# Sine products of the rotation and norm weights of queries and keys on VectorE instead of GpSimd

## The chip, the cores and the metric

The kernel runs on one core of a Trainium2 chip. The metric is the device time of one execution in microseconds, the median of several runs. The engines are TensorE (PE, matmuls; PEld is its weight load), VectorE (DVE), ScalarE (ACT), GpSimd (POOL) and SyncE (SP), which issues the transfers.

## What is computed

Two layers of a hybrid block over 1024 latent tokens and 256 context tokens, width 1024, float32. Each layer norms and modulates its input and projects it with one wide matrix; three mixers work on the result and a second matrix adds their output to the residual. The mixers are differential attention (four heads, two maps of 64 dimensions each, values of 128), a state space scan (16 heads) and a retention scan (4 heads). The two steps that the change touches, cut from the reference:

```
def rms_norm(x, gain):                       # per head and map, over 64 dimensions
    return x * rsqrt(mean(x * x) + EPS) * gain

def apply_rope(x, cos, sin):                 # x1, x2: halves of the last axis
    return concatenate([x1 * cos - x2 * sin, x1 * sin + x2 * cos])

q_l = apply_rope(rms_norm(aq, attn_q_norm), cos, sin)      # attention, per head
k_l = apply_rope(rms_norm(ak, attn_k_norm), cos, sin)
k_c = rms_norm(ak_c, attn_k_norm)                          # context: no rotation
q, k = apply_rope(rq, cos, sin), apply_rope(rk, cos, sin)  # retention: no norm
```

## The kernel before

Tokens lie on partitions in ten tiles of 128 (eight latent, two context). Every dense product is computed in three matmuls: weights and activations are split in a high part (`wh`, `ah`, rounded on ScalarE) and a rest (`wl` on GpSimd, `al` on VectorE or GpSimd; `split`, L280 to 284), and `mm3` (L301 to 312) sums high by high, high by rest and rest by high in one PSUM buffer. There are two such buffers (`ps_mm`), so a third dense tile waits until the first has been copied out. The projection is a generator (`dense_all`, L1332) that yields after each PSUM tile. The mixers are generators too, and `phase` (L392) draws dense tiles between a mixer's steps by a budget per phase, so that TensorE has dense matmuls between the short ones of a mixer. This sets only the order in which instructions are written; a scheduler then reorders them per engine by its own estimate of when each is ready, and each engine runs its list in order.

`two_units` (L342) makes 128 columns each of two units (such as q0 and q1): tile by tile, ScalarE copies the first unit out of PSUM, VectorE the second (`copy`, L118). `head_prep` (L945) takes one head's k and q: `qk_norm` (L931) sums the squares, forms the inverse root on VectorE, multiplies by it (L942) and then by the gain (L943); `rope` (L916) works in two pieces of four tiles: a sine product into `rm` (L924), a cosine product in place (L925), and a difference and a sum of half width (L928, L929). Context tokens are normed but not rotated. Then k is split again (`khl`, L958) and transposed. The first head is prepared in a phase of its own, the next three inside the loop of the head before.

`head_loop` (L1045) runs over blocks of 128 queries. For each of two maps, `head_b` makes the scores (L986), their maxima on VectorE (`mx`, L988), the negated maximum of all (`nb`, L993) and the exponentials on ScalarE (L998); `head_c1` subtracts the second map from the first on VectorE (`rho`, L1013, one element per partition, and the update of `e`, L1016, up to 1280 columns); then follow transposes (L149) and the product with the values (L1037). `ret_mix` (L1108) calls `rope` for rk and rq of two retention heads, four times in all.

GpSimd also makes the rests of the weights (L284), products of the scan (L766, L895, L901) and of retention (L1141, L1167).

Of the kernel before, what the change touches and what calls it, by code (L numbers as in the profile page):

```python
# [13 lines left out]
ALU = mybir.AluOpType  # L14
# [4 lines left out]
P = 128  # L19
# [33 lines left out]
class Net:  # L53
# [862 lines left out]
    def rope(self, x):  # L916
        nc = self.nc
        for i in range(0, NLT, 4):
            t = slice(i, i + 4)
            m = self.work("rm", (P, 4, 4, 32))  # L920
            x4 = x[:, t, :].rearrange("p t (a e) -> p t a e", e=32)
            sb = self.sin[:, t].unsqueeze(2).to_broadcast([P, 4, 4, 32])
            cb = self.cos[:, t].unsqueeze(2).to_broadcast([P, 4, 4, 32])
            nc.gpsimd.tensor_tensor(out=m, in0=x4, in1=sb, op=ALU.mult)  # L924
            nc.vector.tensor_tensor(out=x4, in0=x4, in1=cb, op=ALU.mult)  # L925
            xh = x[:, t, :].rearrange("p t (a s e) -> p t a s e", s=2, e=32)
            mh = m.rearrange("p t (a s) e -> p t a s e", s=2)
            nc.vector.tensor_tensor(out=xh[:, :, :, 0], in0=xh[:, :, :, 0], in1=mh[:, :, :, 1], op=ALU.subtract)  # L928
            nc.vector.tensor_tensor(out=xh[:, :, :, 1], in0=xh[:, :, :, 1], in1=mh[:, :, :, 0], op=ALU.add)  # L929

    def qk_norm(self, x, gain, nt):  # L931
        nc = self.nc
        ss = self.tiny("qss", 2 * NT)
        for i in range(0, nt, 4):
            n = min(4, nt - i)
            sq = self.work("qsq", (P, n, P))
            nc.scalar.activation(out=sq, in_=x[:, i:i + n], func=AF.Square)
            nc.vector.tensor_reduce(out=ss[:, 2 * i:2 * i + 2 * n],
                                    in_=sq.rearrange("p t (m d) -> p (t m) d", m=2), axis=AX.X, op=ALU.add)
        r = self.mean_rsqrt(ss[:, 0:2 * nt], 2 * nt, 64)  # L940
        xv = x[:, 0:nt].rearrange("p t (m d) -> p (t m) d", m=2)
        nc.vector.tensor_tensor(out=xv, in0=xv, in1=r.unsqueeze(2).to_broadcast([P, 2 * nt, 64]), op=ALU.mult)  # L942
        nc.gpsimd.tensor_tensor(out=xv, in0=xv, in1=gain.unsqueeze(1).to_broadcast([P, 2 * nt, 64]), op=ALU.mult)  # L943

    def head_prep(self, h, last):  # L945
        nq = NLT if last else NT
# [619 lines left out]
```

## Time and profile before

| | |
|---|---|
| median of 3 runs | 2859.97 us (2858.49 to 2863.67) |
| profiled execution | 2862.42 us |
| its span in the profile | 2860.6 us, 45098 instructions |
| TensorE busy | 2668.0 us (93%) |
| VectorE busy | 1774.1 us (62%) |
| ScalarE busy | 1058.0 us (37%) |
| GpSimd busy | 775.3 us (27%) |
| mean granted clock of TensorE | 0.964 of full speed |

The span is that of the profiled instructions; the profiled execution took 1.8 us more in all. Times in the rows below are counted from the start of the span. A shape is partitions x elements; buffer numbers are left out of names. A bracket behind a row of a timeline holds the engine's idle time just before it and what ended that.

### The profile page before, as it was taken

The numbers are of one execution on the slowest core, as the hardware profiler recorded it, in microseconds if no ns is written. First come the engines' busy times: TensorE is split into PE (matmuls) and PEld (weight loads), VectorE is DVE, ScalarE is ACT, GpSimd is POOL, SyncE is SP. The second block draws the span as 40 slices with busy tenths as digits, with TensorE's granted clock in tenths as the row PEclk, the third lists the DMA queues.
The fourth block names the chain that finished last, engine by engine and source line by source line (L and its number), as shares of the span: only waits on it lengthen the run. The fifth ranks groups of instructions, "written<-read, shape, count | busy, mean of one in ns | idle before, by whom it ended". The sixth has DMA issues, their size and how long they took to land.

```text
span 2860.6 us, 45098 instructions
## 1 busy us (share of the span) xinstructions
PE 2668.0 (93%) x17116; PEld 2342.0 (82%) x17116; DVE 1774.1 (62%) x4213; ACT 1058.0 (37%) x2678; POOL 775.3 (27%) x688
## 2 busy tenths in 40 slices
PE   7689999999999999998999989998999999999999
PEld 4578877888888799986878777877988888889787
DVE  5567657656677775656455666667567767564651
ACT  3443323224444545332233443332244544442330
POOL 2333323232111121233231423223421221022540
PEclk8789999999999999998999999998999999999999
DMA  6012212222111111123543112112210010002461
GB/s 245 10 46 73 69 48 74 80 69 83 47 58 45 54 30 34 33 91 110 168 166 95 29 48 71 54 50 66 60 30 16 23 29 24 23 18 67 139 210 56
DMA packets 111832, 196.04 MB, mean 69 GB/s; under 512 B 13600, under 2 KB 43104, under 8 KB 111616
## 3 DMA queue, kind: packets, MB, share of 16 engines
q1 hardware_dynamic: 111616, 193.17, 21.2%
q8 instruction: 135, 2.21, 0.3%
q14 instruction: 81, 0.66, 0.1%
HBM read 155.43 MB, written 37.68 MB: 68 GB/s over the span
## 4 chain that ended last, share of the span: by engine, by line
PE 77%; DVE 12%; DMA 4%; ACT 3%; issue 2%; POOL 2%; SPq 0%; DVEq 0%; ACTq 0%; POOLq 0%
PE mm L310 34%; PE mm L312 18%; PE t L149 5%; PE o L1037 4%; PE s L986 4%; PE s L822 2%; PE s L772 2%; DVE mx L988 2%; PE o L815 1%; DMA mr<-mix 1%; PE t L793 1%; ACT e L998 1%; DVE e L1016 1%; PE mm L541 1%; DMA wa<-in_wa_dram 1%
## 5 line engine op out<-in xcount | busy, mean ns | idle before, releaser
L310 PE MATMUL mm<-ah,wh 128*128 128x512 f32 (+1 forms) x1680 | 630.4, 376 | 12.9 <-DVE xr L1234 6.0
L310 PE MATMUL mm<-al,wh 128*128 128x512 f32 (+1 forms) x1680 | 623.9, 371 | 0.9 <-DVE al L284 0.9
L310 PE MATMUL mm<-ah,wl 128*128 128x512 f32 (+1 forms) x1680 | 622.7, 371 | 0.0
L284 POOL TENSOR_TENSOR wl<-raw,wh 128x512 fp32r<-128x512 f32 x224 | 293.6, 1332 | 762.1 <-ACT wh L282 731.9
L312 PE MATMUL mm<-wh,ah 128*128 128x256 f32 x1568 | 454.4, 290 | 8.7 <-DVE q L118 7.0
L312 PE MATMUL mm<-wl,ah 128*128 128x256 f32 x1568 | 449.3, 287 | 0.5 <-POOL wl L284 0.5
L312 PE MATMUL mm<-wh,al 128*128 128x256 f32 x1568 | 448.5, 286 | 0.0
L310 PEld LDWEIGHTS mm<-ah,wh 128*128 128x128 f32 x1680 | 323.0, 192 | 68.7 <-issue 5.6
L310 PEld LDWEIGHTS mm<-ah,wl 128*128 128x128 f32 x1680 | 322.9, 192 | 50.8 <-issue 0.7
L310 PEld LDWEIGHTS mm<-al,wh 128*128 128x128 f32 x1680 | 323.6, 193 | 49.8 <-DVE al L284 1.5
L312 PEld LDWEIGHTS mm<-wh,ah 128*128 128x128 f32 x1568 | 301.7, 193 | 15.3 <-DVE q L118 7.8
L998 ACT ACTIVATE e<-s,nb 128x512 f32<-128x512 f32 (+1 forms) x384 | 232.1, 614 | 200.7 <-DVE nb L993 197.5
L312 PEld LDWEIGHTS mm<-wl,ah 128*128 128x128 f32 x1568 | 301.7, 192 | 3.5 <-POOL wl L284 0.9
L312 PEld LDWEIGHTS mm<-wh,al 128*128 128x128 f32 x1568 | 301.6, 192 | 1.9
L988 DVE TENSOR_REDUCE mx<-s 128x1 f32<-128x512 f32 (+1 forms) x400 | 225.1, 589 | 58.5 <-PE s L986 56.8
L986 PE MATMUL s<-kT,qT 128*128 128x512 f32 (+1 forms) x800 | 217.9, 379 | 16.6 <-ACT e L998 15.2
L282 ACT ACTIVATE wh<-raw 128x512 fp32r<-128x512 f32 x224 | 130.5, 627 | 214.9 <-PE mm L310 88.5
L1037 PE MATMUL o<-v,aT 128*128 128x128 f32 x1312 | 176.7, 277 | 0.4 <-DVE aT L118 0.4
L1037 PEld LDWEIGHTS o<-v,aT 128*128 128x128 f32 x1312 | 165.3, 193 | 5.2 <-DVE mx L988 0.8
L986 PEld LDWEIGHTS s<-kT,qT 128*128 128x128 f32 x800 | 136.2, 195 | 40.3 <-ACT e L998 25.0
L794 ACT ACTIVATE t<-t 128x512 f32<-128x512 f32 x144 | 82.1, 582 | 159.4 <-PE t L793 155.3
L766 POOL TENSOR_TENSOR xw<-xn,dtpk 128x512 f32<-128x512 f32 (+2 forms) x96 | 79.5, 840 | 213.2 <-PE s L772 102.1
(281 smaller groups left out, 4543.0 us busy)
## 6 DMA issues: line engine op xcount, KB each, us to landing
raw<-in_wi_dram SPq DMA_DIRECT2D x176, 256.0 KB
wa<-in_wa_dram SPq DMA_DIRECT2D x48, 512.0 KB
E<-cume SPq DMA_DIRECT2D x144, 128.0 KB
mr<-mix SPq DMA_DIRECT2D x64, 256.0 KB
raw<-in_wo_dram SPq DMA_DIRECT2D x32, 256.0 KB
x<-xr SPq DMA_DIRECT2D x26, 256.0 KB
mix<-cv SPq DMA_DIRECT2D x8, 640.0 KB
mix<-sg SPq DMA_DIRECT2D x8, 640.0 KB
```

Source lines behind the costliest of these rows:

```text
L149: self.nc.tensor.transpose(ps[:, j * P:(j + 1) * P], srcs[i + j], self.ident)
L282: nc.scalar.activation(out=hi, in_=x, func=AF.Copy)
L284: e.tensor_tensor(out=lo, in0=x, in1=hi.bitcast(F32), op=ALU.subtract)
L310: nc.tensor.matmul(ps, lhsT=w, rhs=x, start=st, stop=sp)
L312: nc.tensor.matmul(ps, lhsT=x, rhs=w, start=st, stop=sp)
L766: nc.gpsimd.tensor_tensor(out=xw, in0=xn[:, a:a + m].rearrange("p t (h e) -> p t h e", h=2), in1=self.wend[:, a:a + m, h0:h0 + 2].unsqueez ...
L772: nc.tensor.matmul(ps[:, j * P:(j + 1) * P], lhsT=bn[:, c, :], rhs=xw[:, j].rearrange("p h e -> p (h e)"), start=True, stop=True)
L794: nc.scalar.activation(out=ps, in_=ps, func=AF.Exp)
L986: nc.tensor.matmul(ps[:, 0:n], lhsT=qT[:, 2 * m + s, :], rhs=kT[m][:, t0:t0 + n], start=(s == 0), stop=(s == 1))
L988: nc.vector.tensor_reduce(out=mx[:, ci:ci + 1], in_=ps[:, 0:n], axis=AX.X, op=ALU.max, negate=len(chunks) == 1)
L998: nc.scalar.activation(out=em[:, t0:t0 + n], in_=pss[ci][:, 0:n], func=AF.Exp, bias=nb, accum_out=z[:, 3 * m + ci:3 * m + ci + 1])
L1037: nc.tensor.matmul(po[:, 0:P], lhsT=aT[j], rhs=v[:, j, :], start=(j == b0), stop=(j == NT - 1))
```

## The change

The sine product of `rope` and the gain product of `qk_norm` are issued on VectorE instead of GpSimd. They read and write the same tiles; no other line is edited.

```
             cb = self.cos[:, t].unsqueeze(2).to_broadcast([P, 4, 4, 32])
-            nc.gpsimd.tensor_tensor(out=m, in0=x4, in1=sb, op=ALU.mult)
+            nc.vector.tensor_tensor(out=m, in0=x4, in1=sb, op=ALU.mult)
             nc.vector.tensor_tensor(out=x4, in0=x4, in1=cb, op=ALU.mult)
...
         nc.vector.tensor_tensor(out=xv, in0=xv, in1=r.unsqueeze(2).to_broadcast([P, 2 * nt, 64]), op=ALU.mult)
-        nc.gpsimd.tensor_tensor(out=xv, in0=xv, in1=gain.unsqueeze(1).to_broadcast([P, 2 * nt, 64]), op=ALU.mult)
+        nc.vector.tensor_tensor(out=xv, in0=xv, in1=gain.unsqueeze(1).to_broadcast([P, 2 * nt, 64]), op=ALU.mult)
```

The scheduler writes another order for all engines from the first head on. Three places follow. The first is GpSimd's list where the first head is prepared; `k_726` is that head's k, `wl_5158` the rest of the weights of the next dense tiles, `wl_5193` that of the ones after; rows with a minus stand only before.

```order
 L766 TENSOR_TENSOR xw_4997<-xn_4296,dtpk_503 128x384
-L943 TENSOR_TENSOR k_726_4592<-k_726_4592,keep_269 128x1280
 L284 TENSOR_TENSOR wl_5158<-raw_5159,wh_5157 128x512
 L284 TENSOR_TENSOR wl_5158<-raw_5161,wh_5157 128x512
 L284 TENSOR_TENSOR wl_5158<-raw_5163,wh_5157 128x512
-L924 TENSOR_TENSOR rm_5456<-k_726_4592,sin 128x512
-L924 TENSOR_TENSOR rm_5461<-k_726_4592,sin 128x512
 L284 TENSOR_TENSOR wl_5158<-raw_5165,wh_5157 128x512
 L284 TENSOR_TENSOR wl_5193<-raw_5194,wh_5192 128x512
```

The three products are gone from the list; the fourth split of `wl_5158` follows the third directly.

The second place is VectorE's list there; `q_804` is a unit of q that is being copied out of PSUM. Before:

```order
L118 COPY adar_5176<-mm_5167 128x512
L826 SCALAR_TENSOR_TENSOR cv_3817<-cv_3817,cols_113,o_5106 128x256
L834 TENSOR_TENSOR cv_3817<-cv_3817,s_5107 128x256
L925 TENSOR_TENSOR k_726_4592<-k_726_4592,cos 128x512
L242 SCALAR_TENSOR_TENSOR ada_148<-t_5178,cols_113 128x8
L834 TENSOR_TENSOR cv_3817<-cv_3817,s_5107 128x256
L928 TENSOR_TENSOR k_726_4592<-k_726_4592,rm_5456 128x8x32
L929 TENSOR_TENSOR k_726_4592<-k_726_4592,rm_5456 128x8x32
L925 TENSOR_TENSOR k_726_4592<-k_726_4592,cos 128x512
L284 TENSOR_TENSOR khl_5556<-k_726_4592,khl_5556 128x4x64
L928 TENSOR_TENSOR k_726_4592<-k_726_4592,rm_5461 128x8x32
L929 TENSOR_TENSOR k_726_4592<-k_726_4592,rm_5461 128x8x32
```

The first copy of `q_804` is the row after these. With the change, from the same copy of `adar_5176` on:

```order
L118 COPY adar_5176<-mm_5167 128x512
L924 TENSOR_TENSOR rm_5456<-k_726_4592,sin 128x512
L924 TENSOR_TENSOR rm_5461<-k_726_4592,sin 128x512
L834 TENSOR_TENSOR cv_3817<-cv_3817,s_5093 128x256
L925 TENSOR_TENSOR k_726_4592<-k_726_4592,cos 128x512
L118 COPY q_804_5203<-mm_5204 128x128
L925 TENSOR_TENSOR k_726_4592<-k_726_4592,cos 128x512
L826 SCALAR_TENSOR_TENSOR cv_3817<-cv_3817,cols_113,o_5106 128x256
L928 TENSOR_TENSOR k_726_4592<-k_726_4592,rm_5456 128x8x32
```

Both sine products stand in front, and the first copy of `q_804` stands between the two cosine products instead of behind the rope.

The third place is VectorE's list where the q of head 1 is normed and rotated inside the loop of head 0; `mx_6925` and `nb_6938` are the maxima of one block of scores, `e_6743` the exponentials that the block before updates, `v_1107` a unit that is copied out of PSUM. Before:

```order
L942 TENSOR_TENSOR q_804_5203<-q_804_5203,ry_6713 128x1280
L988 TENSOR_REDUCE mx_6925<-s_6926 128x1
L1007 TENSOR_REDUCE zs_6944<-z_6727 128x2
L988 TENSOR_REDUCE mx_6925<-s_6930 128x1
L118 COPY v_1107_6845<-mm_6846 128x128
L1011 RECIPROCAL rz_6946<-zs_6944 128x2
L118 COPY v_1107_6845<-mm_6897 128x128
L988 TENSOR_REDUCE mx_6925<-s_6934 128x1
L1013 SCALAR_TENSOR_TENSOR rho_6948<-zs_6944,nlam_280,rz_6946 128x1
L993 TENSOR_REDUCE nb_6938<-mx_6925 128x1
L1016 SCALAR_TENSOR_TENSOR e_6743<-e_6826,rho_6948,e_6743 128x1280
L925 TENSOR_TENSOR q_804_5203<-q_804_5203,cos 128x512
```

With the change:

```order
L942 TENSOR_TENSOR q_804_5203<-q_804_5203,ry_6713 128x1280
L988 TENSOR_REDUCE mx_6925<-s_6926 128x1
L943 TENSOR_TENSOR q_804_5203<-q_804_5203,keep_269 128x1280
L1007 TENSOR_REDUCE zs_6944<-z_6727 128x2
L988 TENSOR_REDUCE mx_6925<-s_6930 128x1
L118 COPY v_1107_6845<-mm_6846 128x128
L118 COPY v_1107_6845<-mm_6897 128x128
L988 TENSOR_REDUCE mx_6925<-s_6934 128x1
L924 TENSOR_TENSOR rm_6887<-q_804_5203,sin 128x512
L924 TENSOR_TENSOR rm_6892<-q_804_5203,sin 128x512
L1011 RECIPROCAL rz_6946<-zs_6944 128x2
L993 TENSOR_REDUCE nb_6938<-mx_6925 128x1
```

The gain product stands between the maxima and ahead of both v copies, the sine products ahead of `nb_6938`; behind these rows come the rest of the rope and only then the update of `e_6743`.

## Rows read from the trace of the kernel before

**Rows 1.** The page: busy us, share of the span, instructions of each engine.

```profile
PE 2668.0 (93%) x17116; PEld 2342.0 (82%) x17116; DVE 1774.1 (62%) x4213; ACT 1058.0 (37%) x2678; POOL 775.3 (27%) x688
```

**Rows 2.** The page: the chain that ended last, shares of the span by engine.

```profile
PE 77%; DVE 12%; DMA 4%; ACT 3%; issue 2%; POOL 2%; SPq 0%; DVEq 0%; ACTq 0%; POOLq 0%
```

**Rows 3.** Busy us by stretch: PE, PEld, DVE, ACT, POOL, clock, DMA, GB/s.

```profile
550.00:650.00 100.00, 94.08 (x721) 88.02 (x720) 56.12 (x138) 27.30 (x69) 28.03 (x16) 0.97 0.25 81
650.00:1155.00 505.00, 480.57 (x3447) 432.52 (x3447) 350.91 (x835) 238.63 (x721) 90.82 (x58) 0.98 0.16 51
2100.00:2555.00 455.00, 427.39 (x3032) 393.08 (x3031) 318.00 (x758) 218.94 (x664) 81.22 (x53) 0.98 0.08 24
```

**Rows 4.** VectorE's groups by form, the norm: busy, mean ns.

```profile
L942 DVE TENSOR_TENSOR k<-k,ry 128x1280 f32<-128x1280 f32 x8 | 11.9, 1488 | 0.1
L942 DVE TENSOR_TENSOR q<-q,ry 128x1024 f32<-128x1024 f32 x4 | 4.9, 1222 | 0.1
```

**Rows 5.** The cosine product's line: ns least, median, most; first, last start.

```profile
L925 DVE TENSOR_TENSOR k<-k,cos x16: 670/684/1748, 579.9 to 2363.1; 128x512 f32<-128x512 f32 x16
```

**Rows 6.** GpSimd's groups by form, the moved products: busy, mean ns.

```profile
L943 POOL TENSOR_TENSOR k<-k,keep 128x1280 f32<-128x1280 f32 x8 | 23.6, 2946 | 157.1 <-DVE k L942 73.5 <-PE t L149 38.6 <-DVE nb L993 31.7
L924 POOL TENSOR_TENSOR rm<-q,sin 128x512 f32<-128x512 f32 x16 | 26.6, 1684 | 0.6
```

**Rows 7.** Timelines at 878 us, GpSimd and VectorE: start, us, instruction.

```profile
878.31 3.00 POOL L943 TENSOR_TENSOR q<-q,keep 128x1280 f32<-128x1280 f32 x1 [36.06 <-DVE q L942]
878.41 2.92 DVE L1013 SCALAR_TENSOR_TENSOR rho<-zs,nlam,rz 128x1 f32<-128x1 f32 x1
```

**Rows 8.** VectorE's timeline, the same two lines, GpSimd idle.

```profile
714.54 0.21 DVE L1013 SCALAR_TENSOR_TENSOR rho<-zs,nlam,rz 128x1 f32<-128x1 f32 x1
715.32 1.54 DVE L1016 SCALAR_TENSOR_TENSOR e<-e,rho,e 128x1280 f32<-128x1280 f32 x1
```

**Rows 9.** VectorE's timeline, first and last row on a moved product.

```profile
579.94 1.58 DVE L925 TENSOR_TENSOR k<-k,cos 128x512 f32<-128x512 f32 x1
2552.43 2.65 DVE L1016 SCALAR_TENSOR_TENSOR e<-e,rho,e 128x1280 f32<-128x1280 f32 x1
```

**Rows 10.** VectorE's groups by form, two products of two SBUF inputs.

```profile
L799 DVE TENSOR_TENSOR mt<-mt,t 128x512 f32<-128x512 f32 x72 | 49.2, 684 | 0.4
L284 DVE TENSOR_TENSOR al<-mr,ah 128x512 fp32r<-128x512 f32 x32 | 36.9, 1166 | 14.6 <-ACT ah L282 14.4
```

**Rows 11.** TensorE's timeline, dense tiles of q, idle time in brackets.

```profile
576.64 0.38 PE L312 MATMUL mm<-wh,ah 128*128 128x256 f32 x1 [0.22 <-DVE zu L364]
590.02 0.58 PE L312 MATMUL mm<-wh,ah 128*128 128x256 f32 x1 [5.70 <-DVE q L118]
```

**Rows 12.** VectorE's timeline there.

```profile
585.99 3.10 DVE L284 TENSOR_TENSOR khl<-k,khl 128x256 fp32r<-128x256 f32 x1
589.68 0.28 DVE L118 COPY q<-mm 128x128 f32<-128x128 f32 x1
```

**Rows 13.** GpSimd's timeline there.

```profile
578.44 2.53 POOL L924 TENSOR_TENSOR rm<-k,sin 128x512 f32<-128x512 f32 x2
580.91 4.61 POOL L284 TENSOR_TENSOR wl<-raw,wh 128x512 fp32r<-128x512 f32 x3
```

**Rows 14.** ScalarE's timeline there, the fourth split's first half.

```profile
579.26 0.63 ACT L282 ACTIVATE wh<-raw 128x512 fp32r<-128x512 f32 x1 [4.06 <-DMA raw<-in_wi_dram]
```

**Rows 15.** Busy us behind that stall, columns as in rows 3.

```profile
590.00:599.70 9.70, 9.68 (x61) 9.69 (x62) 2.65 (x9) 4.78 (x12) 5.21 (x3) 0.73 0.31 105
```

**Rows 16.** TensorE's timeline at the rope of rk.

```profile
1312.28 1.12 PE L149 MATMUL t<-ident,rk 128*128 128x128 f32 x4 [4.63 <-DVE rk L929]
```

**Rows 17.** TensorE's timeline, two waits for the e update.

```profile
884.18 0.63 PE L149 MATMUL t<-ident,e 128*128 128x128 f32 x4 [0.76 <-DVE e L1016]
965.58 1.07 PE L149 MATMUL t<-ident,e 128*128 128x128 f32 x8 [2.12 <-DVE e L1016]
```

**Rows 18.** TensorE's timeline at the q of head 1.

```profile
740.79 0.39 PE L312 MATMUL mm<-wh,ah 128*128 128x256 f32 x1 [0.74 <-DVE v L118]
```

## The prediction

> **What bounds the kernel now.** I read the busy times first, then the chain of waits, then the busy times by stretch, and last the timelines at the places where the moved products stand. TensorE is busy for 2668.0 of 2860.6 us, so that 192.6 us are all that any reordering of other engines could give; VectorE follows with 1774.1 us, GpSimd has 775.3 us in all [rows 1]. In the chain that ended last TensorE holds 77%, VectorE 12%, GpSimd 2% [rows 2]. The reader is to see two things in this: GpSimd is not what the kernel waits for, and VectorE is the engine that the change loads and the second on the chain. By stretch: where the first head is prepared (550 to 650 us) TensorE is busy for 94.1 of 100 us; in the head loops of layer 0 for 480.6 of 505 us with VectorE at 350.9, in those of layer 1 for 427.4 of 455 with VectorE at 318.0 [rows 3]. VectorE is thus at 69 to 70% where twelve of the sixteen norms run, and TensorE still idles some 5% there.
>
> **What moves, and its gross price on VectorE.** Sixteen gain products (one per norm of k or q, two layers of four heads) and 48 sine products (two per rope; eight k, eight q, four rk and four rq). The gain product has the form of the line ahead of it: a whole k or q times a broadcast operand. That line takes 1.488 us on 1280 columns and 1.222 us on 1024 [rows 4]; twelve of the first and four of the second make 17.9 + 4.9 = 22.8 us. The sine product has the form of the cosine product, 0.684 us [rows 5]: 48 x 0.684 = 32.8 us. Gross: +55.6 us on VectorE. Off GpSimd go products of 2.95 us and of about 1.3 us each (a mean of 1.68 where they waited) [rows 6]; with GpSimd at 27% this is worth nothing by itself. No DMA is issued by either line, so no queue of transfers is moved; the order that the scheduler writes changes on all engines from the first head on.
>
> **What VectorE gets back.** The profile shows the two engines in each other's way. At 878.31 us GpSimd begins a gain product of 3.00 us; VectorE's next instruction, one element per partition, lasts 2.92 us and ends with it [rows 7]. The same line takes 0.21 us, and the e update behind it 1.54 us, where GpSimd is idle [rows 8]. I went through the VectorE rows that lie on one of the 64 products: 23 of them are longer than their form alone, by 23.2 us together; the first (1.58 for 0.68 us) and the last (2.65 for 1.54 us) are shown [rows 9]. That goes. The Trainium skill, page "SBUF — State Buffer", section "Who interferes with whom", says that a VectorE instruction with two SBUF inputs contends with a GpSimd instruction that reads SBUF, and that the one that comes later waits for the whole of the other; the rows of 878 us agree. By that page the change also has a price: the 64 products have two SBUF inputs on VectorE as well, and meet the weight splits that stay on GpSimd.
> How much the 64 products are held up on VectorE I bound from rows: the sum of two masks (512 columns, two SBUF inputs) means 0.684 us over 72, no stall at all; the splits of the mix loads, made while GpSimd does the same, mean 1.166 us over 32, 0.48 more [rows 10]. So 64 products pay between 0 and 31 us. I take 0.1 us each, 6 us, nearer to the first, since in the head loops GpSimd is left with little (90.8 of 505 us now, the moved products among it [rows 3]). Net on VectorE: 55.6 + 6 - 23 = **+38 us**. If all 64 met a split, the worst that the page's rule allows here, the net were 64 us, and the time by the sum below 2860.
>
> **What of it reaches the end.** Of 38 us I count VectorE's share of the chain, 12%: **+4.6 us**. Bounds: 0, if TensorE's dense matmuls cover all of it, and 18 us, the slower rival below.
>
> **First place, the head prepared at 575 to 590 us.** Here TensorE stands still for 5.70 us until a copy of q frees its PSUM buffer [rows 11]. In the order before, GpSimd has two sine products ahead of the fourth split of the same weights: they occupy it from 578.44 to 580.91, and the split follows at once [rows 13], though its input was on its way from 579.26 [rows 14]. The order on TensorE starts the next q tile while it waits, so both tiles end together, and VectorE reaches the first q copy only behind the cosine products and a split of k that lasts 3.10 us [rows 12]. After the change nothing of the head stands ahead of that split on GpSimd, the first q tile is finished first, and its copy stands between the two cosine products. Worked out: the split's input is ready at 579.26 + 0.63 = 579.9, the split (4.61 / 3 = 1.5 us) at 581.4. A matmul takes 9.7 x 0.73 / 61 = 0.116 us at full clock [rows 15]. TensorE starts the tile at 576.64 [rows 11], has done 18 of its 24 matmuls at 578.7 and waits 2.7 us for the split. In the 13.4 us from 576.64 to 590.02 it works 13.4 - 5.7 = 7.7 us; the same work with the new wait ends at 587.0, when the first copy is long made: **-3.0 us**. Behind the stall the granted clock is 0.73 over 9.7 us [rows 15], so partly at the lower of its two levels (1.2 and 2.4 GHz), which costs 9.7 x 0.27 = 2.6 us; a wait of 2.7 us remains, so I count half: **-1.3 us**.
>
> **Second place, the rope of rk at 1307 to 1312 us.** TensorE waits 4.63 us for the last line of the rope [rows 16], while GpSimd makes sine products. In the new order the sine products stand in front on VectorE, and TensorE's next instructions are dense matmuls that wait for two residual updates instead of the rope. The bounds are 0 and -4.6. I take **-1.0 us**, near 0, because three of the four sine products (0.684 us each) stand ahead of the first of those updates.
>
> **Third place, attention.** Two waits of TensorE for the e update, 0.76 us at 884.18 and 2.12 us at 965.58 [rows 17], lie right behind such hold-ups; I count **-2.0** of their 2.9 us. On the other side the products now stand in front of the softmax. At the q of head 1 the gain product comes between the maxima, and in front of the v copies: TensorE waits there 0.74 us already [rows 18], and that grows by the 1.49 us of the product. The two sine products stand ahead of the negated maximum and the whole rope ahead of the e update, which comes later by at least 1.49 + 4 x 0.684 = 4.2 us, less the stalls that end. Two tiles of dense matmuls (2 x 24 x 0.116 = 5.6 us) stand on TensorE for that time; they start when the v copies are made. The loss is the wait for those copies, at most 1.5 us, and lies inside the 4.6 us above.
>
> **Sum.** -3.0 - 1.3 - 1.0 - 2.0 + 4.6 = -2.7 us. The profiled execution took 2862.4 us (1.8 around its span; 2.45 above the median of the runs, 2859.97): 2859.7 for one like it, and **2857** for the median. What a measurement of this kernel can tell from no change is about 0.2%, 5.7 us.
>
> **Rivals.**
> 1. The softmax pays (slower). The scheduler puts a ready product ahead of the negated maximum and the e update; while GpSimd had them, they ran in the gaps. Twelve norms lie in head loops; if each costs TensorE the 1.49 us of its gain product, that is 18 us in place of 4.6: 2857 + 13 = 2870. From 0.6 us per norm on (7.3 us) the change is slower than before, from 1.1 on by more than 0.2%. For it: the wait at 740.79, VectorE at 70%. Against it: TensorE is 94 to 95% busy in the head loops with dense matmuls to fill in [rows 3].
> 2. The stalls weighed more than I count. Both first places lose their stalls and clock falls whole (5.7 + 2.6 + 4.6), the e waits go (2.9), and VectorE's net load is covered: -16 us, 2844. For it: VectorE's stalls come in the middle of in-order chains. Against it: the new order keeps waits at both places.
> 3. TensorE hides it all, and the first place only changes its wait (weights instead of a PSUM buffer): 2859 to 2861. For it: 93% busy. Against it: 5.7 us of plain idle that the order explains.
> Beside these the order changes in places that have nothing to do with the products; that adds a few us of either sign, which is in the ranges.
>
> **How the numbers follow.** Forecast 0.50, rival 1 0.24, rival 2 0.17, rival 3 0.09. The forecast's own range is 2849 to 2863; about 0.22 of its 0.50 lie below 2854.3, the rest within 0.2%. Rival 2 is faster, rival 1 slower, rival 3 two thirds within and one third slower. Faster 0.39, same 0.34, slower 0.27. The range for 8 in 10 reaches from short of all of rival 2 with favourable reordering, 2839, to just above rival 1, 2872.
>
> **What would show it.** Right: VectorE's busy time near 1812 us, GpSimd's near 660; the one-element line near 0.21 us at all places; no wait of 5 us for a q copy near 585; the rope's wait near 1310 shorter. Wrong: waits of TensorE for v copies, e or the maxima grown by over 10 us in the head loops (rival 1), or VectorE's busy time above 1830 us, its products stalled by the splits. A time above 2866 or below 2849 refutes the sum.

## The result

| | before | after |
|---|---|---|
| median of six runs each, taken together | 2864.3 us (2858.5 to 2866.3) | 2886.6 us (2878.3 to 2891.0) |
| ratio, 95% interval | | 1.0082 (1.0069 to 1.0095) |
| profiled execution; its span | 2862.4; 2860.6 | 2879.3; 2877.5 us |

The change makes the kernel 0.8% slower; 2857 was forecast, and the range ended at 2872. The profiled execution of after is one of its faster ones, so its trace shows 16.9 of the 22 us.

### The profile page after: what moved, and what is told of

It reads as the page before. It is cut to its first block, busy times and chain, and to the rows that moved or that the text cites. A ratio compares the mean times of both kernels' runs of the same rounds, so it can differ in the third digit from the quotient of the medians.

```text
span 2877.5 us, 45074 instructions
## 1 busy us (share of the span) xinstructions
PE 2671.4 (93%) x17116; PEld 2340.5 (81%) x17116; DVE 1793.1 (62%) x4277; ACT 1059.5 (37%) x2678; POOL 659.9 (23%) x624
## 5 line engine op out<-in xcount | busy, mean ns | idle before, releaser
L312 PE MATMUL mm<-wl,ah 128*128 128x256 f32 x1568 | 451.3, 288 | 1.9 <-POOL wl L284 1.9
L986 PE MATMUL s<-kT,qT 128*128 128x512 f32 (+1 forms) x800 | 220.3, 380 | 20.4 <-ACT e L998 18.9
```

What stands on the lines that cost most here:

```text
L312: nc.tensor.matmul(ps, lhsT=x, rhs=w, start=st, stop=sp)
L986: nc.tensor.matmul(ps[:, 0:n], lhsT=qT[:, 2 * m + s, :], rhs=kT[m][:, t0:t0 + n], start=(s == 0), stop=(s == 1))
```

## The profile after

The page's busy times, to be held against [rows 1]:

```profile
PE 2671.4 (93%) x17116; PEld 2340.5 (81%) x17116; DVE 1793.1 (62%) x4277; ACT 1059.5 (37%) x2678; POOL 659.9 (23%) x624
```

VectorE's busy time grew by 19.0 us, not by 38, and GpSimd fell to 660 as forecast. TensorE is busy for 3.4 us more and idle for 13.5 us more, at the same mean granted clock as before, 0.964. The products on VectorE by form (busy us, mean ns), and the one-element line of [rows 7] (ns least, median, most):

```profile
L943 DVE TENSOR_TENSOR k<-k,keep 128x1280 f32<-128x1280 f32 x8 | 11.9, 1483 | 0.0
L924 DVE TENSOR_TENSOR rm<-k,sin 128x512 f32<-128x512 f32 x16 | 10.9, 718 | 0.0
L924 DVE TENSOR_TENSOR rm<-q,sin 128x512 f32<-128x512 f32 x16 | 10.3, 681 | 0.0
```

```profile
L1013 DVE SCALAR_TENSOR_TENSOR rho<-zs,nlam,rz x64: 206/219/222, 644.3 to 2571.8; 128x1 f32<-128x1 f32 x64
```

The products cost what [rows 4, 5] said, hardly anything holds them up (the worst mean is 718 ns, where the same form means 681), and the one-element line is at 0.22 us everywhere. So VectorE is less loaded than I feared. Busy times by stretch, columns as in [rows 3]:

```profile
550.00:650.00 100.00, 96.57 (x722) 87.81 (x721) 61.78 (x148) 28.48 (x70) 18.24 (x11) 0.97 0.25 81
650.00:1155.00 505.00, 473.56 (x3379) 426.85 (x3379) 347.08 (x832) 231.56 (x700) 51.53 (x40) 0.97 0.16 51
2100.00:2555.00 455.00, 424.16 (x2965) 388.56 (x2965) 318.00 (x767) 218.96 (x653) 47.06 (x36) 0.97 0.09 25
```

In the 505 us of layer 0's head loops TensorE does 3379 matmuls where it did 3447. The place is seen on TensorE's timeline (start, us, instruction, idle time before it and what ended that), in the loop of head 2, where the k of head 3 is normed and rotated:

```profile
965.73 1.64 PE L986 MATMUL s<-kT,qT 128*128 128x512 f32 x6 [1.10 <-ACT e L998]
...
971.21 2.08 PE L986 MATMUL s<-kT,qT 128*128 128x512 f32 x4 [3.83 <-ACT e L998]
...
982.98 1.94 PE L149 MATMUL t<-ident,khl 128*128 128x128 f32 x8 [3.21 <-DVE khl L284]
...
995.42 0.39 PE L312 MATMUL mm<-wh,ah 128*128 128x256 f32 x1 [3.27 <-DVE adar L118]
```

Before, there were two such waits here, that of 2.12 us in [rows 17] and this one:

```profile
980.85 2.01 PE L986 MATMUL s<-kT,qT 128*128 128x512 f32 x4 [2.19 <-ACT e L998]
```

VectorE's timeline of after in front of the wait of 3.83 us:

```profile
961.42 0.68 DVE L988 TENSOR_REDUCE mx<-s 128x1 f32<-128x512 f32 x1
962.02 1.47 DVE L943 TENSOR_TENSOR k<-k,keep 128x1280 f32<-128x1280 f32 x1
963.42 0.41 DVE L988 TENSOR_REDUCE mx<-s 128x1 f32<-128x256 f32 x1
...
964.74 1.28 DVE L924 TENSOR_TENSOR rm<-k,sin 128x512 f32<-128x512 f32 x2
965.94 1.28 DVE L925 TENSOR_TENSOR k<-k,cos 128x512 f32<-128x512 f32 x2
967.15 0.41 DVE L928 TENSOR_TENSOR k<-k,rm 128x256 f32<-128x256 f32 x1
967.48 0.41 DVE L929 TENSOR_TENSOR k<-k,rm 128x256 f32<-128x256 f32 x1
967.82 0.67 DVE L988 TENSOR_REDUCE mx<-s 128x1 f32<-128x512 f32 x1
...
970.19 0.15 DVE L993 TENSOR_REDUCE nb<-mx 128x1 f32<-128x3 f32 x1
```

Read alone, this looks like rival 1: products and rope stand ahead of the maxima, the negated maximum is late, and with it the exponentials that free TensorE's score buffers. I took that as theory 1. By TensorE's waits over the whole run (us in total, times, longest), those for the exponentials grew from 15.2 to 18.9 us and those for the negated maximum from 1.4 to 8.1; first before, then after:

```profile
PE s L986 <- ACT e L998: 15.2, 13, 2.2
...
PE t L149 <- DVE nb L993: 1.4, 2, 1.1
```

```profile
PE s L986 <- ACT e L998: 18.9, 15, 3.8
...
PE t L149 <- DVE nb L993: 8.1, 7, 1.7
```

Theory 2: the loss is the order that the scheduler writes on all engines once two lines have other engines, whoever makes the products. Theory 3: VectorE's load, wherever it stands.

At the other places: the first place's wait (5.70 us in [rows 11]) is 3.43 us, the wait at the q of head 1 [rows 18] grew from 0.74 to 1.95, and at the rope of rk the wait of 4.63 [rows 16] is gone. In its place stands one of 3.13 us for a residual update; the one of 3.25 us ahead of it, for another such update, was there before as well:

```profile
587.64 0.58 PE L312 MATMUL mm<-wh,ah 128*128 128x256 f32 x1 [3.43 <-DVE q L118]
...
739.01 0.58 PE L312 MATMUL mm<-wh,ah 128*128 128x256 f32 x1 [1.95 <-DVE v L118]
...
1304.99 0.77 PE L310 MATMUL mm<-ah,wh 128*128 128x512 f32 x1 [3.25 <-DVE xr L1234]
...
1321.60 0.36 PE L310 MATMUL mm<-ah,wh 128*128 128x256 f32 x1 [3.13 <-DVE xr L1234]
```

The first of those two waits in the kernel before:

```profile
1294.91 0.70 PE L310 MATMUL mm<-ah,wh 128*128 128x512 f32 x1 [3.25 <-DVE xr L1234]
```

## The experiments

Ratios are to the kernel before, run beside each on the same chip (its medians there 2859.2 to 2860.4 us). "Length of the loops" is the time from the start of the first e update (L1016) in a layer's head loops to that of the 37th of 40 in layer 0, and to that of the last of 32 in layer 1.

**Part by part.** The engine of each product becomes an argument; only the first head of a layer (`e_first`), only heads 1 to 3 (`e_loop`) or only the retention ropes (`e_ret`) have VectorE. The lines of `e_first`:

```
-        nq = NLT if last else NT
+        nq, ge, se = NLT if last else NT, *((self.nc.vector, self.nc.vector) if h == 0 else (self.nc.gpsimd, self.nc.gpsimd))
```

> Only the first head of each layer (prepared outside the head loops) has its sine and gain products on VectorE; heads 1 to 3 and the retention ropes keep them on GpSimd. Theory 1 (in the head loops the products stand ahead of the softmax on VectorE, and TensorE pays): no loss here, the gain of the first place remains: 2858 to 2865, ratio 0.998 to 1.001. Theory 2 (it is the rewritten order, which moves the time by several us wherever anything changes): any ratio from 0.996 to 1.008, not near 1 by rule. Theory 3 (VectorE's added work counts by its amount wherever it stands): 11.2 of 55.6 us moved, so a fifth of the loss of 23 us, 4.6 us, ratio 1.0016.

> Only heads 1 to 3 of each layer (prepared inside the loop of the head before) have sine and gain products on VectorE. Theory 1: the whole loss or a little more than it, 2884 to 2892, ratio 1.007 to 1.010. Theory 2: any ratio from 0.996 to 1.010. Theory 3: 33.5 of 55.6 us, 14 us, ratio 1.005.

> Only the ropes of the retention mixer have the sine products on VectorE. Theory 1: no softmax beside it, 2860 to 2866, ratio 0.999 to 1.001. Theory 2: any ratio from 0.996 to 1.008. Theory 3: 10.9 of 55.6 us, 4.6 us, ratio 1.0016.

Measured: 0.9989 (0.9979 to 0.9999), 1.0078 (1.0059 to 1.0097), 0.9965 (0.9953 to 0.9977). `e_first` and `e_loop` are where theory 1 had them; `e_ret` is a gain that it did not foresee. Beside them an edit that moves no work:

```
-        for i in range(0, NLT, 4):
+        for i in range(NLT - 4, -1, -4):
```

> Nothing is moved between engines: the rope works on its second piece of four tiles before its first, everywhere, so that the scheduler writes another order. Theory 1: within 0.2% of before, ratio 0.998 to 1.002. Theory 2: off by several us, beyond 0.2% in either direction. Theory 3: ratio 1.000.

Measured 1.0038 (1.0026 to 1.0051): against theory 1 alone. Another order costs 11 us with the same work on the same engines.

**Sum, removal, spacing, priority.** `e_fr` joins `e_first` and `e_ret`. `e_drop` leaves products out (`if ge:` and `if se:` ahead of them, `None` for heads 1 to 3). `e_spread` and `e_soft` start from the changed kernel:

```
-        self.rope(k)
+        self.rope(k, 0)
+        yield
+        self.rope(k, 4)
...
-                e0 = self.head_b(qTs[i], kT, 0, z, ch[i])
+                with self.tc.high_priority(offset=300): e0 = self.head_b(qTs[i], kT, 0, z, ch[i])
```

(the same for q, a `yield` ahead of the gain product in `e_spread`; the same for the second `head_b` and `head_c1` in `e_soft`).

> Sine and gain products on VectorE for the first head of each layer and in the retention ropes, on GpSimd for heads 1 to 3. Theory 1 (only products among the softmax cost): the two gains add up, ratio 0.9989 x 0.9965 = 0.9954, about 2847 us. Theory 2 (each new order is a draw of its own, about 0.4% either way): anything from 0.992 to 1.004, the two runs before it say nothing of this one.

> As before, but heads 1 to 3 leave their sine and gain products out altogether (their q and k lack the norm weight, and the rotation takes x itself in place of the sine product), so neither engine makes them. It shows what taking them off GpSimd gives by itself. Theory 1: the removal alone is worth a few us (hold-ups of VectorE end, the chain of each norm is shorter), ratio 0.994 to 1.000; so the 22 us of e_loop come from putting them on VectorE. Theory 2: as much off as any new order, 0.996 to 1.008. If it is as slow as e_loop (1.006 or more), the loss comes from the GpSimd side or from the order, and theory 1 falls.

> All products on VectorE as in the changed kernel, but the preparation of a head is handed out in smaller steps: the gain product, and each of the two pieces of a rope, stand in a step of their own, one step per block of queries (10 steps for 10 blocks in place of 6). Theory 1 in the form that the burst of norm and rope on VectorE holds up one block's softmax: most of the loss goes, ratio to the kernel before 0.996 to 1.002. If VectorE's load in the head loops is what counts, whatever the burst: 1.006 to 1.009, as after. Theory 2: anything from 0.996 to 1.010.

> All products on VectorE as in the changed kernel, but scores, maxima, exponentials and the e update of the head loops are given a higher priority (by 300 instructions) in the scheduler, so that it puts them ahead of a norm or rope that is ready at the same time. Theory 1: a good part of the loss goes, ratio to before 0.997 to 1.004. Theory 2 or plain load: 1.004 to 1.012.

Measured: `e_fr` 1.0028 (1.0018 to 1.0037), `e_drop` 1.0022 (1.0012 to 1.0032), `e_spread` 1.0093 (1.0080 to 1.0106), `e_soft` 1.0049 (1.0033 to 1.0065). Two gains that should add up to 0.9954 give a loss, so theory 1 does not even carry from one run to the next, and the burst form of theory 1 misses with `e_spread`; `e_soft` lies where theory 2 or plain load would have it. `e_drop` tells most: its head loops of layer 0 are 15 us longer than before, with no product on either engine for heads 1 to 3, and its waits stand where those of after do:

```profile
977.33 1.40 PE L986 MATMUL s<-kT,qT 128*128 128x512 f32 x4 [1.94 <-ACT e L998]
988.43 1.48 PE L149 MATMUL t<-ident,khl 128*128 128x128 f32 x8 [2.71 <-DVE khl L284]
...
1001.06 0.39 PE L312 MATMUL mm<-wh,ah 128*128 128x256 f32 x1 [3.02 <-DVE adar L118]
```

That the products are on VectorE cannot be the reason for these.

**Order held.** To part order and engine, I held each engine's list to a given order by ties between neighbours that only bind the order of issue:

```
+    for code in HELD.values():               # one list of instructions per engine
+        ...
+            if last is not None:
+                tc.add_manual_dep(by[name], last, why, reason="order")
+            last = name
```

`o_b_vec` is the changed kernel in the order of before; `o_a_gps` is the kernel before in the order of after; a moved product takes the place that it has in the scheduler's whole list. `o_b_drop` is `e_drop` in the order of before. `p_flip_v` makes the change in `p_flip`, nothing held. In the traces of `o_b_vec` and of before TensorE's instructions stand in the same sequence by line and tile, and so they do in those of `o_a_gps` and of after.

> The products are on VectorE as in the changed kernel, but every engine is held to the order of the kernel before; each product stands in VectorE's list at the place that it had in the scheduler's whole list when GpSimd made it. Theory 1 (products on VectorE hold up the softmax): most of the loss is still here, ratio 1.004 to 1.009. Theory 2 (the loss is the order that the scheduler writes for the new engines): no loss, ratio 0.994 to 1.001. Theory 3 (VectorE's load): as theory 1, VectorE's busy time being the same.

> The other way round: the products are on GpSimd as in the kernel before, but every engine is held to the order that the scheduler wrote for the changed kernel. Theory 1 and 3: the loss is gone, ratio 0.998 to 1.002. Theory 2: the loss is here as well, ratio 1.006 or more (the products' longer time on GpSimd can add to it).

> Heads 1 to 3 leave out their sine and gain products, as in e_drop, but every engine is held to the order of the kernel before. It is what the products on GpSimd cost where no order changes. With e_drop at 1.0022, theory 2 expects less here: 0.993 to 1.000. If it is 1.002 again, the loss of e_drop was not the order.

> The change made to p_flip in place of the kernel before (rope works on its second piece first, all products on VectorE), with an order of its own. Theory 1 and 3: 0.8% above p_flip, ratio to before about 1.012. Theory 2: a draw of its own, 0.998 to 1.010, not tied to p_flip's 1.0038.

| | order of before | order of after |
|---|---|---|
| products on GpSimd | 1 | 1.0043 (1.0030 to 1.0056) |
| products on VectorE | 1.0012 (1.0003 to 1.0022) | 1.0082 (1.0069 to 1.0095) |

`o_b_drop` is at 0.9991 (0.9979 to 1.0003), `p_flip_v` at 1.0067 (1.0054 to 1.0080), where theories 1 and 3 had about 1.012. Theory 2 holds, though for half of the loss only (1.0043, short of the 1.006 that I had put down for it). Theory 1 fails for the order of before, where the same work on VectorE costs 0.12%, and theory 3 with it: VectorE is busy for 1795.8 us in `o_b_vec` and for 1793.1 in after. Holding an order costs nothing that shows: `o_b_ret` below, a part of the change in the order of before, is at 1.0003. The waits of after stand in `o_a_gps` too, though GpSimd makes its products:

```profile
976.84 1.89 PE L986 MATMUL s<-kT,qT 128*128 128x512 f32 x4 [4.31 <-ACT e L998]
988.34 1.94 PE L149 MATMUL t<-ident,khl 128*128 128x128 f32 x8 [3.30 <-DVE khl L284]
...
1001.72 0.58 PE L312 MATMUL mm<-wh,ah 128*128 128x256 f32 x1 [3.00 <-DVE adar L118]
```

In `o_b_vec` the products do hold up the e update once (5.24 us, 2.12 in [rows 17]), and the waits behind it, that for khl at 976.57 and that for adar at 988.81 us, are short (that for the exponentials between them is 2.18 us, as before):

```profile
965.42 1.94 PE L149 MATMUL t<-ident,e 128*128 128x128 f32 x8 [5.24 <-DVE e L1016]
976.57 1.06 PE L149 MATMUL t<-ident,khl 128*128 128x128 f32 x8 [0.59 <-DVE khl L284]
...
988.81 0.39 PE L312 MATMUL mm<-wh,ah 128*128 128x256 f32 x1 [0.29 <-DVE adar L118]
```

Length of the loops in the profiled executions, layer 0 and layer 1:

| order | kernel: products | layer 0, us | layer 1, us |
|---|---|---|---|
| before | before: GpSimd | 501.2 | 449.7 |
| before | `o_b_vec`: VectorE | 504.4 | 451.8 |
| before | `o_b_drop`: none in heads 1 to 3 | 500.8 | 449.2 |
| after | `o_a_gps`: GpSimd | 516.1 | 451.3 |
| after | after: VectorE | 513.7 | 455.8 |
| own | `e_drop`: none in heads 1 to 3 | 516.5 | 445.7 |
| own | `e_loop`: VectorE in heads 1 to 3 | 517.7 | 454.9 |
| own | `p_flip`; `p_flip_v` | 498.2; 515.6 | 453.0; 457.6 |
| own | `e_soft`: VectorE, softmax ahead | 506.4 | 460.1 |
| own | `e_spread`: VectorE, smaller steps | 510.3 | 464.9 |
| own | `e_first`; `e_fr`; `e_ret`: GpSimd in heads 1 to 3 | 505.2; 506.3; 501.3 | 449.4; 451.9; 448.9 |

In layer 0 the length goes with the order, not with the engine: 501 to 504 us in one, 514 to 516 in the other. Nor does the long one look like a chance draw. Where the scheduler was free, the six kernels with no product left on GpSimd in heads 1 to 3 have 506.4 to 517.7 us, the five that keep them there 498.2 to 506.3. The lower two of the six, `e_soft` and `e_spread`, pay for it in layer 1. Each length is from one execution; that of `e_soft` was its slowest. How a length is read, with VectorE's rows of `o_a_gps` (1166.14 - 650.01 = 516.1):

```profile
650.01 1.54 DVE L1016 SCALAR_TENSOR_TENSOR e<-e,rho,e 128x1280 f32<-128x1280 f32 x1
...
1166.14 1.55 DVE L1016 SCALAR_TENSOR_TENSOR e<-e,rho,e 128x1280 f32<-128x1280 f32 x1
```

**Where in the order.** The two orders have the same instructions behind them at many points, so one can be spliced into the other.

> All products on VectorE; every engine is held to the order of o_b_vec (1.0012), except in the four head loops of layer 0 (650 to 1151 us of the kernel before), where it is held to the order of the changed kernel. If the loss is the order of these loops: the lags of the traces over this stretch (+13.4 us for after, +4.5 for o_b_vec) give 9 us more than o_b_vec, ratio 1.004 to 1.005. If the loss is spread over the program: 1.002 to 1.003. If each splice is a draw of its own: anything.

> As s_loop0, but the order of the changed kernel stands only from 869 to 1018 us (the loop of head 2, in which the k of head 3 is normed and rotated). Local theory: 6.5 us more than o_b_vec by the lags, ratio 1.003 to 1.004, with the waits for the exponentials, khl and adar near 970 to 1000 us. Spread theory: 1.001 to 1.002.

> The reverse of s_loop0: the order of the changed kernel everywhere, except in the head loops of layer 0, where the order of o_b_vec stands. All products on VectorE. Local theory: 9 us less than after (1.0082), ratio 1.004 to 1.006. If the head loops of layer 0 were the whole loss: 1.000 to 1.002. Spread theory: 1.006 to 1.008.

> Only the sine products of the retention ropes are on VectorE (as e_ret, 0.9965), with every engine held to the order of the kernel before. If the engine gives the gain: the lags of o_b_vec over the two retention stretches (-4.2 and -2.6 us) give 7 us, ratio 0.997 to 0.998. If e_ret's gain is its order: 0.9995 to 1.001.

Measured: `s_loop0` 1.0062 (1.0046 to 1.0079), `s_h2` 1.0042 (1.0028 to 1.0057), `s_rest` 1.0039 (1.0024 to 1.0054), `o_b_ret` 1.0003 (0.9991 to 1.0015). All three splices lie nearest to the local theory: the figures are just outside its ranges (`s_loop0` and `s_h2` above, `s_rest` below), the intervals reach into them, and none reaches into a range of the spread theory. Layer 0's head loops carry 0.50% going in and 0.43% coming out, the loop of head 2 alone 0.30%, the rest of the order 0.27%. `s_h2` against `o_b_vec`, busy us over the spliced stretch (columns as in [rows 3]), first `o_b_vec`, then `s_h2`:

```profile
869.00:1020.00 151.00, 140.85 (x1010) 127.27 (x1009) 114.20 (x275) 67.57 (x206) 10.90 (x8) 0.98 0.14 47
```

```profile
869.00:1020.00 151.00, 137.64 (x913) 122.44 (x912) 102.04 (x242) 62.51 (x189) 10.34 (x8) 0.91 0.14 47
```

TensorE is idle for 3.2 us more, and its granted clock is 0.91 for 0.98. By an estimate, 140.85 x 0.98 = 138.0 us of work at full clock are done in the one and 137.64 x 0.91 = 125.3 in the other, 12.8 us less; the 27th e update of the layer comes at 1028.79 us in the one and at 1016.58 in the other, from like starts. Of the 12.8 us the idle time takes 3.2 and the clock the rest, some 9.6. In `s_h2` the waits are those of after, within 0.2 us:

```profile
973.25 2.08 PE L986 MATMUL s<-kT,qT 128*128 128x512 f32 x4 [3.83 <-ACT e L998]
...
984.98 1.94 PE L149 MATMUL t<-ident,khl 128*128 128x128 f32 x8 [3.30 <-DVE khl L284]
...
998.36 0.58 PE L312 MATMUL mm<-wh,ah 128*128 128x256 f32 x1 [3.01 <-DVE adar L118]
```

The granted clock is down at each of them or right behind it:

```profile
970.00:975.00 5.00, 1.75 (x4) 1.34 (x5) 4.56 (x11) 1.91 (x6) 0.00 (x0) 0.54 0.10 39
985.00:990.00 5.00, 5.00 (x20) 4.51 (x21) 3.06 (x8) 2.39 (x7) 0.00 (x0) 0.50 0.00 0
1000.00:1005.00 5.00, 5.00 (x28) 5.00 (x26) 0.17 (x1) 0.90 (x2) 0.00 (x0) 0.55 0.00 0
```

So `s_h2` has 0.79 from 960 to 990 us and 0.87 to 1020, where `o_b_vec` has 0.89 and 1.00; first `s_h2`, then `o_b_vec`:

```profile
960.00:990.00 30.00, 21.97 (x126) 17.67 (x125) 25.05 (x51) 12.11 (x37) 2.14 (x2) 0.79 0.35 123
990.00:1020.00 30.00, 26.79 (x189) 25.50 (x188) 17.86 (x43) 13.34 (x42) 0.00 (x0) 0.87 0.00 1
```

```profile
960.00:990.00 30.00, 21.43 (x140) 19.08 (x139) 24.80 (x51) 14.68 (x45) 5.21 (x4) 0.89 0.34 120
990.00:1020.00 30.00, 29.65 (x238) 28.47 (x237) 24.68 (x62) 14.10 (x45) 0.00 (x0) 1.00 0.00 1
```

Not all of the 9.6 us goes with the order. About 3 are a fall of the clock to 0.70 from 920 to 930 us, behind waits of 1.15 and 0.62 us for weights; after has waits of 0.70 and 0.62 us there and a clock of 1.00 from 869 to 940. From 940 to 1020 us the order does show in the clock: before, then after, then `o_a_gps`:

```profile
940.00:1020.00 80.00, 73.61 (x537) 66.53 (x536) 65.08 (x151) 40.10 (x122) 17.70 (x10) 0.98 0.15 49
```

```profile
940.00:1020.00 80.00, 68.18 (x466) 60.71 (x465) 60.92 (x141) 36.64 (x111) 5.02 (x4) 0.91 0.14 49
```

```profile
940.00:1020.00 80.00, 67.64 (x437) 59.39 (x435) 58.00 (x125) 35.21 (x106) 10.58 (x7) 0.89 0.14 48
```

`o_b_ret` takes back what `e_ret` seemed to show: in the order of before, VectorE for the retention ropes gives nothing.

**A faster order.** Two runs put the order of `e_ret` under all products on GpSimd and under all on VectorE.

> All products on GpSimd as in the kernel before; every engine is held to the order that the scheduler wrote for e_ret (0.9965). If e_ret's gain is its order: 0.996 to 0.998, faster with no work moved at all. If it is the engine of the retention ropes: 0.999 to 1.002.

> All products on VectorE as in the changed kernel; every engine is held to the order of e_ret. If the order decides, and VectorE's products cost the 0.12% that they cost in the order of before: 0.997 to 0.999, so the change itself is faster than before in this order. If VectorE's load in the head loops costs what after lost: 1.003 to 1.006.

Measured: `o_r_gps` 0.9967 (0.9955 to 0.9980), 2848.7 us, with no work moved at all; `o_r_vec` 0.9989 (0.9978 to 1.0000). The first is the kernel before with another order, and with `e_ret` the fastest here; the second is the change itself, now not slower than before. VectorE's share is 0.22% in this order, 0.12% in that of before and 0.39% in that of after.

## Why the prediction was wrong

- **The step that failed** is the sentence "Beside these the order changes in places that have nothing to do with the products; that adds a few us of either sign". Measured with the engines as before, the new order costs 0.43%, 12 us, and for the change as it is the order of before saves 0.70%, 20 us. I read the new order at the three places where I looked for gains, and costed no other. By the traces layer 0's loops are 12.4 us longer: 5.9 us up to the 22nd e update, 9.9 from there to the 27th, in the loop of head 2, and 3.4 made good behind it. Nor has that place nothing to do with the products: the k of head 3 is normed and rotated there. Every sign that I had named for "right" came, but for VectorE's busy time, and so did the sign against the sum, a time above 2866. The signs for "right" tested the places that I had worked out, and none of them the order elsewhere.
- **The load on VectorE (+4.6)** was about right for one order, and that by luck. In the order of before the two sets of head loops are longer by 3.2 and 2.1 us with the products on VectorE, 5.3 us in all and 0.44 us per norm: less than rival 1's 1.49. But 4.6 was 12% of a net load of 38 us, and 12% of the 21.7 us measured in that order is 2.6. Over the whole program the products cost 0.12% there, 3.4 us, and in the two other orders 0.22% and 0.39%, 6 and 11 us: no one price, as the sum assumed.
- **VectorE's busy time (+38 net)** was too high. The gross +55.6 is right (54.6 us in after); regained were 36 us, not 23, and the new hold-ups that I set at 6 are below 1 in after (718 ns for 681 over 16 sine products of k) and about 2.5 in `o_b_vec` (832 ns for 684). The Trainium skill, page "SBUF — State Buffer", section "Who interferes with whom", has the rule behind the old hold-ups, that the later of two contending instructions waits for the whole of the other; the traces agree: the one-element row that lasted 2.92 us [rows 7] is at 0.22 at most with GpSimd's products gone. The price that I had drawn from it hardly came. (For its worst case the sum gives 2860.3, not a time below 2860.)
- **First place (-3.0 and -1.3):** the wait fell by 2.3 us, and from 560 to 645 us after gains about 1.3 us on before, by the columns that TensorE has done. Right mechanism, a third of the size.
- **Second place (-1.0):** in the held order the rope's wait fell from 4.63 to 1.79 us. In after it gave way to a wait of 3.13 us for a residual update: 1.5 us gained, near the -1.0. I had written that TensorE would wait for two such updates instead of the rope; the wait for the other, 3.25 us, was there before as well.
- **Third place (-2.0):** the hold-ups of the e update went, as said; but this is the stretch (965 to 1003 us) where the new order puts four waits and the clock falls. I had quoted its first wait [rows 17] as a gain. In the order of before, with the products on VectorE, that wait grew from 2.12 to 5.24 us. The wait for the v copies grew by 1.2 us in after and by 1.4 in `o_b_vec`, within the 1.5 that I gave it.
- **Rival 1** had the sign and the loops. Its mechanism, "if each costs TensorE the 1.49 us of its gain product", is not what the loss is made of: `e_drop` and `o_a_gps` lose 15 us in layer 0's loops without a product on VectorE in heads 1 to 3. Nor did its sign come in full: the waits for the exponentials, the e update, the v copies and the negated maximum grew from 21.7 to 30.8 us together, not by over 10, and they are at 28.0 in `o_a_gps`.

Open: which instructions of that loop make the order bad. No run parts VectorE's list from TensorE's in the spliced stretch. `o_a_gps` loses 0.43% and after 0.82%; 11 us between them are VectorE's products in that order, of which the traces show 3.5, both at a mean granted clock of 0.964. The rest goes with the clock of the other executions: the mean over six is 0.965 for `o_a_gps` and 0.960 for after, whose profiled execution has its highest. What lowers it there is not shown.

## What to carry to other kernels

Where a scheduler writes the order, an edit is two changes, the work and a new order, and at 93% TensorE the second can be the larger: three other orders of the very same work gave 0.9967, 1.0038 and 1.0043. Before a loss of under 1% is put down to an engine, hold the order and move the work, then hold the work and move the order. And do not add up gains of two edits that were each measured with an order of its own.

## What was not expected of the hardware

A few more short waits can cost TensorE more by the clock than by themselves: in `s_h2` 3.2 us of extra idle time came with a mean granted clock of 0.91 in place of 0.98 over 151 us, by an estimate 9.6 us of work, of which some 3 us come with a fall of the clock that after does not have. From 940 to 1020 us the kernels in the order of after are at 0.87 to 0.91 (after, `o_a_gps`, `s_loop0`, `s_h2`), those in the order of before at 0.96 to 0.98 (before, `o_b_vec`, `o_b_drop`). Over the whole of the profiled execution of after the clock is not lower than before, 0.964 in both; its 16.9 us there are 13.5 us of idle and 3.4 us of busy time.
